# Logarithms and exponentials of the stick-breaking mixer: each kind behind the whole of the other, in a program ordered by its own planner

## The chip, the cores and the metric

The kernel runs on one core of a Trainium2 chip. The metric is the device time of one execution in microseconds, the median of several runs. The engines are PE (TensorE, matrix products, PEld its weight loads), DVE (VectorE, elementwise), ACT (ScalarE, functions by table, and copies), POOL (GpSimd, hardly used) and SP (SyncE, which issues the transfers). Each engine takes its instructions in the order of its own list.

## The reference

A trunk of two layers over 256 positions of width 1024. Each layer is a SwiGLU block, a mixer, and a second SwiGLU block, each with a residual and a layer norm. The mixer of layer 0 is a recurrence (RWKV-7); that of layer 1 is stick-breaking attention over 12 heads. Both are joined with attention over 256 memory tokens. The part that the change touches:

```python
for blk in range(seq // Q_BLOCK):            # two blocks of 128 queries
    ...
    z = jnp.einsum('bhtd,bhsd->bhts', q[:, :, start:end], kb).astype(jnp.float32) * scale
    ...
    log_keep = jnp.where(before, -jax.nn.softplus(z), 0.0)
    later = lax.cumsum(log_keep, axis=3, reverse=True) - log_keep
    att = jnp.where(before, jnp.exp(jax.nn.log_sigmoid(z) + later), 0.0)
    outs.append(jnp.einsum('bhts,bhsd->bhtd', att.astype(v.dtype), vb))
```

All is float32.

## The kernel before

**Tiling.** The 256 positions are two halves of 128, one per partition. Weights arrive by SP in pieces of 128 x 1024 (512 KB, tiles `raw`). ACT copies each piece to fp32r (`hi`), DVE subtracts to get the rest (`lo`), and a product is made of three PE instructions of 512 columns: hi x hi, hi x lo, lo x hi. The activations are held turned in `xTh` and `xTl`. Ten `raw`, nine `hi` and nine `lo` buffers go round. One half's mixer runs beside SwiGLU work of the other half, so that PE has wide products to do while the mixer's chain is on ACT and DVE.

**The stick-breaking mixer** (function `stick`, called once per half). The first half has one block of keys (the diagonal one), the second has two. Scores `z` go to the tiles `qr` (diagonal block) and `Sk` (earlier block). The softplus is taken as max(z, 0) + ln(1 + exp(-|z|)), in tiles of two pairs of heads' scores, 128 x 768: `L` and `Lm` for the diagonal block, `T` and `Tt` for the earlier one. So there are two such tiles in the first half and four in the second, and for each one: ACT takes the absolute value, ACT takes exp(-x) (the *first exponential*), ACT takes ln(1 + x) (the *logarithm*), DVE combines it with the scores (a SCALAR_TENSOR_TENSOR). Then, in groups of 384 columns, PE sums along the keys by a product with a triangular constant (`cst` in the lists), in the second half plus a product with ones of the diagonal block's tile, into the two PSUM banks `ps_2r` and `ps_3r` (tag `tp`); DVE subtracts that from the scores in place; ACT takes the exponential in place (the *last exponential*). Last come the products with the values (`gup_108r`, `vn`), and then the products with `w_out`.

**What sets the order.** The program is recorded first and ordered afterwards, by the class `Plan`. `order` is a list scheduler: each instruction has a price, and at each step it takes for some engine the ready instruction of lowest rank. For ACT it keeps which table is loaded, by the list `SETS` of line 119: an instruction whose function is not in the present set is ranked later by `SWITCH` (line 426) and priced 1300 ns more (line 438). `latest` works due times from the end backwards, and `improve` repeats both 24 times with random shakes of the due times and keeps the best by the planner's own sum. So the prices of one place can change the order of the whole program. Which table each instruction then really needs is settled later, when the program is built, and there a load (ACT_TABLE_LOAD) is put ahead of an instruction whose function the loaded table lacks.

In `stick`, `x.after` lists instructions that have to stand ahead of `x`. Before the change each logarithm stands behind `done`, the last of the half's first exponentials in the order of recording (line 1358), and each last exponential behind `ln`, the last recorded logarithm.

All instructions are issued from line 599, so rows are told apart by their tiles (`L_374r` is the tile `L`, `qr_408r` the scores of the diagonal block). In the lists `ps_` are PSUM banks, `h` the SwiGLU's gated values, `hT` these values turned.

Of the kernel before, what the change touches and what calls it, by code (L numbers as in the profile page):

```python
# [16 lines left out]
AF = mybir.ActivationFunctionType  # L17
# [98 lines left out]
        return lambda *a, **k: self.plan.add(self.name, getattr(self.real, method), method, a, k)  # L116


SETS = (("Exp", "Tanh"), ("Sigmoid", "Tanh"), ("Ln", "Exp"), ("Silu", "Tanh"))
LINK = 45.0  # L120
AGAIN = 32.0
LAND = 3200.0
# [8 lines left out]
class Plan:  # L131
# [214 lines left out]
    def order(self, given=()):  # L346
# [50 lines left out]
        while done < len(ops):  # L397
# [25 lines left out]
            def rank(x):  # L423
                t, o = x
                p = o.pri + (t - t_e) * WAIT
                if e == "ACT" and o.func and o.func not in SETS[table]:
                    p += SWITCH
# [9 lines left out]
            took = o.took  # L437
            if e == "ACT" and o.func and o.func not in SETS[table]:
                table = next(i for i, s in enumerate(SETS) if o.func in s)
                took += 1300.0  # L440
# [162 lines left out]
def kernel(ctx, tc, const, x, mem, f1g, f1u, f1d, f2g, f2u, f2d, ln_g, ln_b, w_out, w_mem_kv,  # L603
                      rw_in, r_mu, r_w0, r_wup, r_a0, r_aup, r_gup, r_kk, r_ka, r_rk, r_lng, r_lnb, sb_in, out):
    nc = Plan(tc.nc)
# [8 lines left out]
    def new(pool, shape, dtype, tag, name, bufs=1):  # L614

        return nc.slot(pool, shape, dtype, tag, nm(name), bufs)

    def ps(tag):
        return new(psp, [P, 512], F32, tag, "ps", 2)
# [9 lines left out]
    def bc(ap, axis, shape):  # L629
        return ap.unsqueeze(axis).to_broadcast(shape)  # L630
# [44 lines left out]
    def split_T(src_ps, dst, j0, n):  # L675

        hi, lo = dst
        sp = src_ps[:, :n * P].rearrange("p (k t) -> p k t", t=P)
        nc.scalar.activation(hi[:, j0:j0 + n], sp, AF.Copy)
        nc.vector.tensor_sub(lo[:, j0:j0 + n], sp, hi[:, j0:j0 + n].bitcast(F32))  # L680
# [209 lines left out]
    def sl(n, shape=None):  # L890
        return new(mp, shape or [P, MIX], F32, n, n)

    def project(hf, w, c0, n):

        a = ps("gu")
        run(cols_mm(a[:, :n], xT[hf], cols_pieces(w, c0, n)))
        t = new(tp_, [P, n], F32, "ta", "pn", 2)
        nc.copy(t, a[:, :n])
        return t

    def turned(src, i0, n):
        pt = ps("tp")
        with nc.together():
            for i in range(n):
                nc.tensor.transpose(pt[:, i * P:(i + 1) * P], src[:, (i0 + i) * P:(i0 + i + 1) * P], ident)
        return pt[:, :n * P].rearrange("p (i t) -> p i t", t=P)
# [396 lines left out]
    def stick(hf, res):  # L1303
        ac = f"acc{hf}"
        qT = sl("bn", [P, NT, P])
        if hf == 0:
            kT = new(cp, [P, NT, P], F32, "S", "kT0")
            V = new(cp, [P, MIX], F32, "gup", "V0")
        else:
            kT, V = sl("kn", [P, NT, P]), sl("vn")  # L1310
        B[hf] = kT, V
        t = project(hf, sb_in[0], 2048, 512)
        nc.copy(V[:, 512:768], t[:, 0:256])
        mq = new(mp, [P, 2, P], F32, "mq", "mq")
        nc.copy(mq, turned(t, 2, 2), 0.125)
        yield "p"
        t = project(hf, sb_in[0], 0, 512)
        nc.copy(qT[:, 0:4], turned(t, 0, 4), 0.125)
        yield "p"
        t = project(hf, sb_in[0], 512, 512)  # L1320
        tv = turned(t, 0, 4)
        nc.copy(qT[:, 4:6], tv[:, 0:2], 0.125)
        nc.copy(kT[:, 0:2], tv[:, 2:4])
        yield "p"
        t = project(hf, sb_in[0], 1024, 512)
        nc.copy(kT[:, 2:6], turned(t, 0, 4))
        yield "p"
        t = project(hf, sb_in[0], 1536, 512)
        nc.copy(V[:, 0:512], t)
        yield "p"  # L1330
        mem_attention(hf, mq)
        zs, sps = {}, {}
        v3 = lambda t: t.rearrange("q (i t) -> q i t", i=3)
        for si, ts in enumerate(range(hf, -1, -1)):
            zm = zs[ts] = sl("qr" if si == 0 else "Sk", [P, 4, 384])
            sps[ts] = [sl(n, [P, 2, 384]) for n in (("L", "Lm") if si == 0 else ("T", "Tt"))]
            for jg in range(2):
                banks = [ps(ac) for _ in range(2)]
                with nc.together():
                    for i in range(3):  # L1340
                        for p in range(2):
                            pr, j = slice(p * HD, (p + 1) * HD), 3 * jg + i
                            nc.tensor.matmul(banks[p][:, i * P:(i + 1) * P], B[ts][0][pr, j], qT[pr, j], start=True, stop=True)
                for p, z in enumerate(banks):
                    g = 2 * jg + p
                    if ts == hf:
                        nc.vector.tensor_tensor(v3(zm[:, g]), v3(z[:, :384]), bc(K_("neg"), 1, [P, 3, P]), ALU.add)
                    else:
                        nc.copy(zm[:, g], z[:, :384])
                    yield "z0"  # L1350
                e, zz = sps[ts][jg], zm[:, 2 * jg:2 * jg + 2]
                nc.scalar.activation(e, zz, AF.Abs)
                done = nc.scalar.activation(e, e, AF.Exp, scale=-1.0)
                yield "z1"
        for ts in zs:
            for jg in range(2):
                e, zz = sps[ts][jg], zs[ts][:, 2 * jg:2 * jg + 2]
                ln = nc.scalar.activation(e, e, AF.Ln, bias=1.0)
                ln.after.append(done.i)
                nc.vector.scalar_tensor_tensor(e, zz, 0.0, e, ALU.max, ALU.add)  # L1360
            yield "ln"
        for ts in zs:
            for g in range(4):
                zm = zs[ts][:, g]
                cu = ps("tp")
                nc.tensor.matmul(cu[:, :384], K_("tri"), sps[ts][g // 2][:, g % 2], start=True, stop=ts == hf)
                if ts != hf:
                    nc.tensor.matmul(cu[:, :384], K_("ones"), sps[hf][g // 2][:, g % 2], start=False, stop=True)
                nc.vector.tensor_sub(zm, zm, cu[:, :384])
                nc.scalar.activation(zm, zm, AF.Exp).after.append(ln.i)  # L1370
                yield "e0"
                yield "e1"
        tss = sorted(zs)
        for g in range(2):
            o = ps(ac)
            ov = o[:, :384].rearrange("p (i t) -> p i t", i=3)
            yield "o"
            with nc.together():
                for i in range(3):
                    for ts in tss:  # L1380
                        for p in range(2):
                            h = 6 * g + 2 * i + p
                            nc.tensor.matmul(ov[p * HD:(p + 1) * HD, i], B[ts][1][:, h * HD:(h + 1) * HD],
                                             zs[ts][:, 2 * g + p, i * P:(i + 1) * P], start=ts == tss[0], stop=ts == tss[-1])
            split_T(o, xT[hf], 3 * g, 3)
        res.append(None)
# [45 lines left out]
    for hf in range(NHALF):  # L1432
        xs[hf] = xp.tile([P, D], F32, tag=f"x{hf}", name=nm("x"))
        nc.in_turn("load", nc.sync.dma_start(xs[hf], x[0, half_sl(hf), :]))
        turn_x(hf)
    for i in range(DEPTH):
        mixer, steps = ((rwkv, RW), (stick, SB))[i % 2]
        last = i == DEPTH - 1
        lag1, lag2 = LAGS[i]
# [60 lines left out]
```

## Time and profile before

| | |
|---|---|
| median of 3 runs | 1111.25 us (1110.56 to 1112.19) |
| the profiled execution's own time | 1110.33 us |
| its span, first to last instruction | 1108.5 us |
| PE busy | 1068.3 us (96%) |
| DVE busy | 928.6 us (84%) |
| ACT busy | 760.0 us (69%) |
| table loads on ACT | 19, 24.4 us, 1283 ns each |
| mean granted clock of PE | 0.988 |
| read from HBM | 301.08 MB, mean 273 GB/s |

A row of a timeline has the start in us, the time it took, the engine, the instruction with what it writes and reads, how often it stands in a row, and in brackets the idle time of that engine before it and what ended it. Starts of PE's instructions that follow each other closely overlap: the distance of two starts is what an instruction costs PE. The granted clock is the share of 2.4 GHz that PE was given: 1.00 is 2.4 GHz, 0.50 is 1.2 GHz.

### The profile page before, as it was taken

The numbers are of one execution on the slowest core, as the hardware profiler recorded it, in microseconds if no ns is written. First come the engines' busy times: TensorE is split into PE (matmuls) and PEld (weight loads), VectorE is DVE, ScalarE is ACT, GpSimd is POOL, SyncE is SP. The second block draws the span as 40 slices with busy tenths as digits, with TensorE's granted clock in tenths as the row PEclk, the third lists the DMA queues.
The fourth block names the chain that finished last, engine by engine and source line by source line (L and its number), as shares of the span: only waits on it lengthen the run. The fifth ranks groups of instructions, "written<-read, shape, count | busy, mean of one in ns | idle before, by whom it ended". The sixth has DMA issues, their size and how long they took to land.

```text
span 1108.5 us, 17727 instructions
## 1 busy us (share of the span) xinstructions
PE 1068.3 (96%) x6265; PEld 862.6 (78%) x6265; DVE 928.6 (84%) x1312; ACT 760.0 (69%) x1027; POOL 2.7 (0%) x14
## 2 busy tenths in 40 slices
PE   7999999998799999999999999999999998999996
PEld 6878888876687778778888888888867876888885
DVE  6578677999999999998789865659899878997777
ACT  6466556986379785686667654538988899866652
POOL 0000000000000000000000000000000000000000
PEclk9999999999999999999999999999999998999998
DMA  9499758865678687799979976758979975999881
GB/s 330 158 360 383 255 211 293 294 211 195 192 236 315 206 282 251 242 319 364 329 264 368 346 230 201 220 172 303 373 249 333 344 252 189 384 371 304 267 286 58
DMA packets 212250, 303.30 MB, mean 274 GB/s; under 512 B 13844, under 2 KB 159424, under 8 KB 212162
## 3 DMA queue, kind: packets, MB, share of 16 engines
q1 hardware_dynamic: 212162, 302.18, 79.9%
q8 instruction: 49, 0.80, 0.3%
q14 instruction: 39, 0.32, 0.1%
HBM read 301.08 MB, written 1.05 MB: 273 GB/s over the span
## 4 chain that ended last, share of the span: by engine, by line
PE 79%; DVE 11%; ACT 4%; DMA 3%; issue 2%; SPq 0%; DVEq 0%; ACTq 0%
PE ps_30r L599 25%; PE ps_29r L599 23%; PE ps_27r L599 7%; PE ps_28r L599 6%; PE ps_25r L599 6%; PE ps_26r L599 6%; PE ps_2r L599 3%; PE ps_3r L599 3%; DVE x L599 1%; DVE Y_369r L599 1%; DVE lo_44r L599 1%; DMA raw_21r<-in_ffn_w_up_dram 1%; DVE lo_17r L599 1%; ACT L599 1%; DVE lb_498r L599 1%
## 5 line engine op out<-in xcount | busy, mean ns | idle before, releaser
L599 ACT ACTIVATE h_31r<-ps_30r 128x256 f32<-128x256 f32 (+1 forms) x38 | 16.5, 435 | 18.5 <-PE ps_30r L599 18.3
L599 ACT ACTIVATE h_32r<-ps_29r 128x256 f32<-128x256 f32 (+1 forms) x38 | 16.2, 425 | 18.9 <-PE ps_29r L599 18.9
L599 ACT ACT_TABLE_LOAD x19 | 24.4, 1283 | 1.1 <-PEq L1488 0.7
L599 PE MATMUL ps_30r<-hi_10r,xTh 128*128 128x512 f32 (+1 forms) x60 | 23.6, 393 | 0.0
L599 PE MATMUL ps_30r<-hi_10r,xTl 128*128 128x512 f32 (+1 forms) x60 | 23.0, 383 | 0.0
L599 PE MATMUL ps_30r<-lo_11r,xTh 128*128 128x512 f32 (+1 forms) x60 | 22.9, 382 | 0.0
L599 PE MATMUL ps_29r<-hi_16r,xTh 128*128 128x512 f32 x56 | 22.8, 407 | 0.0
L599 PE MATMUL ps_30r<-hi_22r,xTh 128*128 128x512 f32 x56 | 22.8, 406 | 0.0
L599 ACT ACTIVATE h_32r<-ps_30r 128x256 f32<-128x256 f32 (+1 forms) x19 | 7.7, 406 | 21.7 <-PE ps_30r L599 21.7
L599 PE MATMUL ps_30r<-hi_13r,xTh 128*128 128x512 f32 x54 | 22.0, 408 | 0.0
L599 PE MATMUL ps_30r<-hi_22r,xTl 128*128 128x512 f32 x56 | 21.9, 391 | 0.0
L599 PE MATMUL ps_29r<-hi_16r,xTl 128*128 128x512 f32 x56 | 21.9, 391 | 0.0
L599 PE MATMUL ps_29r<-lo_17r,xTh 128*128 128x512 f32 x56 | 21.9, 391 | 0.0
L599 PE MATMUL ps_30r<-lo_23r,xTh 128*128 128x512 f32 x56 | 21.8, 390 | 0.0
L599 PE MATMUL ps_30r<-lo_14r,xTh 128*128 128x512 f32 x54 | 21.2, 392 | 0.4 <-DVE lo_14r L599 0.4
L599 PE MATMUL ps_30r<-hi_13r,xTl 128*128 128x512 f32 x54 | 21.2, 393 | 0.0
L599 PE MATMUL ps_29r<-hi_10r,xTh 128*128 128x512 f32 x52 | 21.2, 408 | 0.0
L599 PE MATMUL ps_29r<-lo_44r,xTh 128*128 128x512 f32 x50 | 19.8, 396 | 1.3 <-DVE lo_44r L599 1.3
L599 PE MATMUL ps_2r<-cst,x 128*128 128x128 f32 x48 | 8.9, 315 | 12.6 <-DVE x L599 7.0
L599 PE MATMUL ps_30r<-hi_7r,xTh 128*128 128x512 f32 x50 | 20.7, 414 | 0.0
L599 PE MATMUL ps_29r<-hi_19r,xTh 128*128 128x512 f32 x52 | 20.6, 397 | 0.0
L599 PE MATMUL ps_30r<-lo_17r,xTh 128*128 128x512 f32 x50 | 19.6, 392 | 0.9 <-DVE lo_17r L599 0.9
(1886 smaller groups left out, 4073.1 us busy)
## 6 DMA issues: line engine op xcount, KB each, us to landing
raw_45r<-in_ffn_w_down_dram SPq DMA_DIRECT2D x17, 512.0 KB, 5.8
raw_24r<-in_ffn_w_down_dram SPq DMA_DIRECT2D x16, 512.0 KB, 5.0
raw_15r<-in_ffn_w_down_dram SPq DMA_DIRECT2D x16, 512.0 KB, 5.0
raw_21r<-in_ffn_w_down_dram SPq DMA_DIRECT2D x15, 512.0 KB, 5.8
raw_39r<-in_ffn_w_gate_dram SPq DMA_DIRECT2D x30, 256.0 KB, 4.6
raw_39r<-in_ffn_w_up_dram SPq DMA_DIRECT2D x30, 256.0 KB, 4.4
raw_42r<-in_ffn_w_gate_dram SPq DMA_DIRECT2D x30, 256.0 KB, 5.1
raw_42r<-in_ffn_w_up_dram SPq DMA_DIRECT2D x30, 256.0 KB, 6.1
```

What stands on the lines that cost most here:

```text
L599: fn(*[at(x) for x in a], **{n: at(x) for n, x in k.items()})
```

## The change

The third entry of `SETS` loses the exponential, so that the planner counts a table switch between a logarithm and an exponential. Every logarithm now stands behind all first exponentials of its half, and every last exponential behind all logarithms of its half.

```diff
-SETS = (("Exp", "Tanh"), ("Sigmoid", "Tanh"), ("Ln", "Exp"), ("Silu", "Tanh"))
+SETS = (("Exp", "Tanh"), ("Sigmoid", "Tanh"), ("Ln",), ("Silu", "Tanh"))
...
-        zs, sps = {}, {}
+        zs, sps, first, logs = {}, {}, [], []
...
                 nc.scalar.activation(e, zz, AF.Abs)
-                done = nc.scalar.activation(e, e, AF.Exp, scale=-1.0)
+                first.append(nc.scalar.activation(e, e, AF.Exp, scale=-1.0).i)
...
-                ln = nc.scalar.activation(e, e, AF.Ln, bias=1.0)
-                ln.after.append(done.i)
+                logs.append(nc.scalar.activation(e, e, AF.Ln, bias=1.0))
+                logs[-1].after += first
...
-                nc.scalar.activation(zm, zm, AF.Exp).after.append(ln.i)
+                nc.scalar.activation(zm, zm, AF.Exp).after += [o.i for o in logs]
```

What it makes of the order, at three places. The first is ACT in the second half of the stick-breaking mixer, layer 1, before the change, from the first table load of that stage on. The rows are the logarithm of `L`, the first exponential of `Lm`, the absolute value of `T`, the logarithm of `Lm`, the first exponential of `T` and the logarithm of `Tt`:

```order
L599 ACT_TABLE_LOAD
L599 ACTIVATE L_374r<-L_374r 128x768
L599 ACT_TABLE_LOAD
L599 ACTIVATE Lm_359r<-Lm_359r 128x768
L599 ACTIVATE hT_1994r<-ps_3r 128x256
L599 ACTIVATE T_368r<-Sk_373r 128x768
L599 ACT_TABLE_LOAD
L599 ACTIVATE Lm_359r<-Lm_359r 128x768
L599 ACT_TABLE_LOAD
L599 ACTIVATE T_368r<-T_368r 128x768
L599 ACT_TABLE_LOAD
L599 ACTIVATE Tt_358r<-Tt_358r 128x768
```

And of the changed program, from the same load on; the four in-place rows of 768 are the four logarithms, the last row the first three of the last exponentials:

```order
L599 ACT_TABLE_LOAD
L599 ACTIVATE L_374r<-L_374r 128x768
L599 ACTIVATE hT_1994r<-ps_2r 128x256
L599 ACTIVATE Lm_359r<-Lm_359r 128x768
L599 ACTIVATE T_368r<-T_368r 128x768
L599 ACTIVATE hi_10r<-raw_45r 128x1024
L599 ACTIVATE Tt_358r<-Tt_358r 128x768
L599 ACTIVATE hi_16r<-raw_42r 128x1024
L599 ACTIVATE hi_19r<-raw_18r 128x1024
L599 ACT_TABLE_LOAD
L599 ACTIVATE h_31r<-ps_30r 128x256
L599 ACTIVATE qr_408r<-qr_408r 128x384 x3
```

The first exponentials of `Lm` and `T` and the absolute value of `T` have moved ahead of the load, and the four logarithms stand together.

The second place is DVE beside it, before the change, from the combine of `L` on (`qr_408r<-qr_408r,ps_2r` is the subtraction that empties a bank):

```order
L599 SCALAR_TENSOR_TENSOR L_374r<-qr_408r,L_374r 128x768
L599 TENSOR_TENSOR hT_1994r<-ps_3r,hT_1994r 128x256
L599 SCALAR_TENSOR_TENSOR Lm_359r<-qr_408r,Lm_359r 128x768
L599 SCALAR_TENSOR_TENSOR Tt_358r<-Sk_373r,Tt_358r 128x768
L599 TENSOR_TENSOR qr_408r<-qr_408r,ps_2r 128x384
L599 SCALAR_TENSOR_TENSOR h_32r<-h_32r,ps_30r 128x256
L599 TENSOR_TENSOR qr_408r<-qr_408r,ps_3r 128x384
```

And of the changed program:

```order
L599 SCALAR_TENSOR_TENSOR L_374r<-qr_408r,L_374r 128x768
L599 TENSOR_TENSOR hT_1994r<-ps_2r,hT_1994r 128x256
L599 SCALAR_TENSOR_TENSOR Lm_359r<-qr_408r,Lm_359r 128x768
L599 SCALAR_TENSOR_TENSOR T_368r<-Sk_373r,T_368r 128x768
L599 TENSOR_TENSOR lo_11r<-raw_45r,hi_10r 128x1024
L599 TENSOR_TENSOR qr_408r<-qr_408r,ps_3r 128x384
L599 TENSOR_TENSOR qr_408r<-qr_408r,ps_2r 128x384
L599 SCALAR_TENSOR_TENSOR Tt_358r<-Sk_373r,Tt_358r 128x768
```

The combine of `Tt` has moved behind the first two subtractions, and the combine of `T` and a weight piece stand ahead of them.

The third place is PE in the first half of layer 0's mixer, where `bn_434r` and then `Lm_359r` are turned (products with `cst`, here the identity) through the same two banks, before the change:

```order
L599 MATMUL ps_2r<-cst,bn_434r 128x128 x4
L599 MATMUL ps_30r<-hi_40r,xTh 128x512
L599 MATMUL ps_30r<-lo_41r,xTh 128x512
L599 MATMUL ps_30r<-hi_40r,xTl 128x512
L599 MATMUL ps_2r<-cst,bn_434r 128x128 x2
L599 MATMUL ps_2r<-cst,Lm_359r 128x128 x4
```

And of the changed program:

```order
L599 MATMUL ps_26r<-qr_408r,bn_434r 64x128
L599 MATMUL ps_2r<-cst,bn_434r 128x128 x6
L599 MATMUL ps_2r<-cst,Lm_359r 128x128 x4
L599 MATMUL ps_3r<-cst,Lm_359r 128x128 x2
L599 MATMUL ps_2r<-cst,h_31r 128x128 x2
```

The three wide products between the first four and the last two transposes of `bn_434r` have moved ahead of them.

## Rows read from the trace of the kernel before

**Rows 1.** The page: busy time, share of the span and instructions of each engine.
```profile
PE 1068.3 (96%) x6265; PEld 862.6 (78%) x6265; DVE 928.6 (84%) x1312; ACT 760.0 (69%) x1027; POOL 2.7 (0%) x14
```

**Rows 2.** Waits of PE: who waited for whom, us in total, times, longest.
```profile
PE ps_2r L599 <- DVE qr_408r L599: 5.0, 1, 5.0
PE ps_3r L599 <- DVE L_374r L599: 2.6, 1, 2.6
```

**Rows 3.** Timeline of ACT, 904 to 927 us: start, us, instruction.
```profile
904.35 1.28 ACT L599 ACT_TABLE_LOAD   x1
905.65 0.85 ACT L599 ACTIVATE L_374r<-L_374r 128x768 f32<-128x768 f32 x1
906.51 1.28 ACT L599 ACT_TABLE_LOAD   x1
907.81 0.85 ACT L599 ACTIVATE Lm_359r<-Lm_359r 128x768 f32<-128x768 f32 x1
...
915.29 0.84 ACT L599 ACTIVATE Tt_358r<-Tt_358r 128x768 f32<-128x768 f32 x1
...
926.35 1.35 ACT L599 ACTIVATE qr_408r<-qr_408r 128x384 f32<-128x384 f32 x3
```

**Rows 4.** Timeline of DVE, 906 to 924 us.
```profile
906.53 0.96 DVE L599 SCALAR_TENSOR_TENSOR L_374r<-qr_408r,L_374r 128x768 f32<-128x768 f32 x1
...
916.16 0.96 DVE L599 SCALAR_TENSOR_TENSOR Tt_358r<-Sk_373r,Tt_358r 128x768 f32<-128x768 f32 x1 [3.35 <-ACT Tt_358r L599]
917.04 0.55 DVE L599 TENSOR_TENSOR qr_408r<-qr_408r,ps_2r 128x384 f32<-128x384 f32 x1
...
923.02 1.22 DVE L599 TENSOR_TENSOR lo_38r<-raw_18r,hi_37r 128x1024 fp32r<-128x1024 f32 x1
```

**Rows 5.** Timeline of PE, both halves of the stick-breaking mixer.
```profile
826.45 1.65 PE L599 MATMUL ps_3r<-L_374r,cst 128*128 128x384 f32 x2 [2.57 <-DVE L_374r L599]
...
910.49 0.81 PE L599 MATMUL ps_2r<-L_374r,cst 128*128 128x384 f32 x2
...
917.64 1.65 PE L599 MATMUL ps_2r<-Lm_359r,cst 128*128 128x384 f32 x2 [5.01 <-DVE qr_408r L599]
...
923.96 0.81 PE L599 MATMUL ps_3r<-T_368r,cst 128*128 128x384 f32 x2
924.60 0.81 PE L599 MATMUL ps_3r<-L_374r,cst 128*128 128x384 f32 x2
...
935.25 0.40 PE L599 MATMUL ps_27r<-hi_40r,xTh 128*128 128x512 f32 x1
```

**Rows 6.** Stretches: length; PE, PEld, DVE, ACT, POOL busy; clock; DMA share, GB/s.
```profile
826.40:832.00 5.60, 5.34 (x20) 2.73 (x20) 5.04 (x15) 4.13 (x6) 0.00 (x0) 0.72 0.03 10
912.60:917.60 5.00, 0.03 (x1) 0.00 (x0) 1.63 (x3) 4.93 (x6) 0.00 (x0) 0.73 0.00 0
917.60:922.30 4.70, 4.66 (x10) 3.23 (x11) 2.64 (x5) 4.25 (x5) 0.00 (x0) 0.56 0.00 0
940.00:1000.00 60.00, 60.00 (x273) 49.32 (x272) 56.44 (x71) 45.51 (x54) 0.00 (x0) 1.00 1.04 377
255.90:259.20 3.30, 3.20 (x8) 2.24 (x9) 3.30 (x4) 0.61 (x2) 0.00 (x0) 0.54 0.59 197
```

**Rows 7.** Timeline of PE, 888.4 to 889.5 us: after two transposes, wide products.
```profile
888.87 0.48 PE L599 MATMUL ps_30r<-hi_13r,xTh 128*128 128x512 f32 x1
889.18 0.40 PE L599 MATMUL ps_30r<-lo_14r,xTh 128*128 128x512 f32 x1
889.42 0.40 PE L599 MATMUL ps_30r<-hi_13r,xTl 128*128 128x512 f32 x1
```

**Rows 8.** Timeline of PE, 251 to 255 us, first half of layer 0's mixer.
```profile
251.56 0.60 PE L599 MATMUL ps_2r<-cst,bn_434r 128*128 128x128 f32 x4
...
252.85 0.44 PE L599 MATMUL ps_2r<-cst,bn_434r 128*128 128x128 f32 x2
254.55 0.66 PE L599 MATMUL ps_2r<-cst,Lm_359r 128*128 128x128 f32 x4 [1.27 <-ACT kn_338r L599]
```

## The prediction

> **What bounds the kernel now.** I read the page first: TensorE (PE) is busy 96% of the span, the other engines less [rows 1]. So a change pays only where PE itself waits, or where its clock falls. Second, PE's waits: the longest one inside the layers that is not the start or a norm is 5.0 us, for DVE's subtraction into `qr_408r`; a smaller one of its kind is 2.6 us, for `L_374r` [rows 2]. Both stand in the stick-breaking mixer, the larger in its second half, the smaller in its first. Third, the timelines of ACT, DVE and PE around the larger wait.
>
> The reader is to see a chain there. ACT loads a table at 904.35, takes the logarithm of `L_374r` at 905.65, and then changes tables again and again: in 904 to 926 us 8 loads like that of 904.35 stand, 1.28 us each [rows 3], of 19 in the kernel. DVE obeys its own order: it has the combine of `L_374r` at 906.53, but the subtraction from `ps_2r` stands behind the combine of `Tt_358r`, whose logarithm comes only after four more loads, at 915.29; so the combine starts at 916.16 and the subtraction at 917.04 [rows 3, 4]. PE, which needs that bank for `Lm_359r`, stands from 912.6 to 917.64 [rows 2, 5]. In that stretch nothing is transferred, and the granted clock is 0.56 from 917.6 to 922.3 [rows 6], which is 1.2 GHz for most of it, after the idle time; then it is 2.4 GHz again.
>
> **The change part by part.** No instruction that computes is added or removed. The two lists only bind the order: all four logarithms of a half behind all its first exponentials, all last exponentials behind all logarithms, and the planner now counts a switch between the two. ACT and DVE are in order, so no new semaphore wait is needed. The first half had its two loads already and keeps them. In the second half the new order has 2 loads where the old had 8 (19 to 13 in all): 6 x 1.28 = 7.7 us less on ACT, about 8 with the start of the following instruction, since 904.35 to 905.65 is 1.30. On ACT alone this is worth nothing; its worth is the PE wait.
>
> *Term 1, the place itself.* From the first product with `L_374r` at 910.49 to the first product of `w_out` at 935.25 PE has the same 52 rows in both orders (3732 to 3783), so the work is equal and only waiting and clock can differ. The wait is 5.0. In 917.64 to 922.34 PE does two pairs of products of 384 columns and six of 512: at full clock 2 x 0.64 (923.96 to 924.60, rows 5) and 6 x 0.23 (889.18 to 889.42 is 0.24, rows 7), 2.7 us; it took 4.7, so the clock cost 2.0 [rows 5 to 7]. Together 7.0 us.
>
> What is late next? In the new order three ACT operations of 768 columns that stood between the loads (the exponential of `Lm_359r` at 907.81, the absolute value and the exponential of `T_368r`) come ahead of the first load. ACT had no idle time there, so the load slips by 3 x 0.84 = 2.5 us to 906.9. I walk on with durations of rows 3 and 4: logarithm of `L_374r` done at 909.0, DVE's combine (0.96) at 910.1, PE there at 910.5: no wait, with 0.4 us to spare. PE then does two pairs (1.3) and six wide products (1.4) and wants the bank for `Lm_359r` at 913.2. DVE now has ahead of the subtraction the combines of `Lm_359r` and `T_368r` and one weight piece `lo_11r` (1.22, as 923.02), which needs its ACT copy: done at 913.4, subtraction (0.55) at 914.0. PE waits 0.8. Further on every pair of banks has three wide products and another pair ahead of it (0.7 + 1.3 us) against one subtraction and one piece on DVE (0.55 + 1.22), so I add only 0.1: 7.0 - 0.9 = 6.1 us gained. Bounds: 7.0 if nothing stays. The nearest row on the other side is the first half, which has two loads only and still waits 2.6, with the clock at 0.72 in 826.4 to 832.0 [rows 2, 5, 6], that is 5.6 x 0.28 = 1.6 lost: if the second half became like it, the gain is 7.0 - 4.2 = 2.8. I take the walk: in the first half PE came to `L_374r` at 823.9 (826.45 less the wait) with nothing left to do, here it is busy up to 910.5 and has six wide products behind the first two pairs.
>
> Behind the subtractions DVE's weight pieces are queued, and for those SP waits with its next loads. In the old order the transfers had stopped by 912.6 (0 GB/s, rows 6); in the new one the piece `lo_11r` frees a buffer at about 913, so the weights of the next block come no later.
>
> *Term 2, fewer changes of kind on PE.* The planner orders the whole program anew; PE differs from its row 203 on. PE's list changes between fp32 and the split fp32r products 333 times instead of 359: 13 fewer returns. A return costs 889.18 - 888.87 - 0.23 = 0.08 us [rows 7]: 1.0 us gained. Bounds 0 and 1.5 (four entries into another tile shape fewer, 0.1 each).
>
> *Term 3, a new wait.* In layer 0's first half the transposes of `bn_434r` were parted by three wide products, which hid ACT's copy: 251.56 the first four, 252.85 the last two [rows 8]. In the new order all six follow each other, the last two into the bank that the copy still reads. Four take 0.35, so PE would wait from 251.9 to 252.85: 0.9 us lost, beside the 1.3 at 254.55 that stays. Bounds: 0, if ACT comes sooner, and 2.5 if the low clock that follows there (0.54 over 3.3 us, rows 6) lasts as long again.
>
> Other places are dealt anew too: PE's waits in layer 0's mixers are small, like the 1.3 of rows 8, and I count no net change, +-2 us.
>
> Sum: -6.1 - 1.0 + 0.9 = -6.2 us. The profiled execution took 1110.33, the median of the runs is 1111.25; the terms are differences, so I take them from the median: 1105.1 us (1104.1 against the profiled one).
>
> **A rule that speaks against it.** The rows show a load at 906.51 between the logarithm at 905.65 and the exponential at 907.81 [rows 3]. The Trainium skill, "ScalarE: Activation LUTs", Table sets, says that a logarithm followed by an exponential needs one load, since one set has both. By that rule there would be no load to save here. The trace does not agree: it has a load where the rule asks for none.
>
> **The rivals.** First, the place stays half blocked: the first logarithm comes later than my walk by more than its 0.4 us, and PE waits for `L_374r` as in the first half. For it: ACT is full ahead of 904.35. Against: PE has the wide products. Gain 2.8 + 1.0 - 0.9 = 2.9: 1108.3.
>
> Second, the weights become the limit and the gain is given back: in 940 to 1000 us the transfer engines are at 1.04 of their time and 377 GB/s [rows 6]. If PE, now ahead by 6 us, drains the buffers there, it waits that long: 1111.2, no change. Against: PE has no wait there in the trace, and loads also start sooner.
>
> Third, the change doesn't do what it says: the loads between the logarithms and the exponentials come from something else than the mixed order, and none goes: -1.0 + 0.9, 1111.2. Against: the load of rows 3 between the two kinds, and 13 loads in the new list. The rule above would give this case.
>
> Fourth, slower: one new gap in layer 0's first half. If the wait of term 3 and those behind it (254.55) leave PE idle long enough that the clock stays at 1.2 GHz through the transposes and small products that follow, each 2 us of that work cost 1 more. The rows show 3.3 us of it after 255.9. It decides from some 17 us on (8.5 lost, against 6.2 + 2.2); at 25 us the time is 1105.1 + 12.5 = 1117.6. Against: wide products follow there.
>
> Fifth, better: the transposes of layer 0 cost nothing, neither the new 0.9 nor the old 1.3, nor the low clock behind them (3.3 x 0.46 = 1.5): 3.7 more, 1101.4. For it: ACT's list is dealt anew there. Against: the six in a row.
>
> **How the numbers follow.** Forecast 0.69, with its own range 1102 to 1108; first rival 0.13, weights 0.05, no effect 0.02, slower 0.05, better 0.06. The range 1101 to 1110 takes in the forecast, the better case and the half-blocked one, and leaves out about 0.12. About 0.2% (2.2 us) is what a measurement can tell from no change. Faster: 0.69 + 0.06 + 0.10 of the 0.13 = 0.85. Same: 0.05 + 0.02 + 0.03 = 0.10. Slower: 0.05.
>
> **What would show it.** Right: 13 table loads; in the second half two, with some 12 us from the first to the first last exponential, where it was 22 (904.35 to 926.35); no PE wait over 1.2 us for `qr_408r`, and a full clock there; a new wait of about 0.9 us for ACT's `kn_338r` near 252. Wrong: a PE wait of 2 us or more for `L_374r` near 910; PE waits for `lo` pieces that wait for transfers in the last 170 us; new waits in layer 0 that sum to more than 4 us.

## The result and the profile after

The changed kernel takes 1101.93 us (median of 4 runs, 1101.54 to 1103.93), the kernel before on the same chip 1110.90 (4 runs, 1109.28 to 1112.19): a ratio of 0.9924, 95% interval 0.9905 to 0.9942. That is 9.0 us faster, where 6.2 were forecast; 1101.93 lies inside the range of 1101 to 1110. The profiled execution spans 1099.8 us, where it was 1108.5.

The page's first lines, engine by engine busy time, share of the span and instructions [rows 1]:

```profile
span 1099.8 us, 17711 instructions
PE 1062.8 (97%) x6265; PEld 861.4 (78%) x6265; DVE 928.8 (84%) x1312; ACT 751.6 (68%) x1021; POOL 2.7 (0%) x14
```

DVE's work is the same; ACT has 8.4 us less, 7.7 of it six table loads, which stand in one row (count, total us, mean ns), where the kernel before had 19 with 24.4 us:

```profile
L599 ACT ACT_TABLE_LOAD x13 | 16.7, 1283 | 0.9 <-PEq L1488 0.7
```

The place is the second half of the stick-breaking mixer. ACT's timeline from the load that stood at 904.35 in [rows 3]:

```profile
904.24 1.28 ACT L599 ACT_TABLE_LOAD   x1
905.54 0.85 ACT L599 ACTIVATE L_374r<-L_374r 128x768 f32<-128x768 f32 x1
906.29 0.37 ACT L599 ACTIVATE hT_1994r<-ps_2r 128x256 fp32r<-128x256 f32 x1
906.55 0.84 ACT L599 ACTIVATE Lm_359r<-Lm_359r 128x768 f32<-128x768 f32 x1
907.29 0.84 ACT L599 ACTIVATE T_368r<-T_368r 128x768 f32<-128x768 f32 x1
...
908.97 0.83 ACT L599 ACTIVATE Tt_358r<-Tt_358r 128x768 f32<-128x768 f32 x1
...
911.71 1.28 ACT L599 ACT_TABLE_LOAD   x1
913.01 0.38 ACT L599 ACTIVATE h_31r<-ps_30r 128x256 f32<-128x256 f32 x1
913.29 1.34 ACT L599 ACTIVATE qr_408r<-qr_408r 128x384 f32<-128x384 f32 x3
```

The logarithm of `Lm` follows that of `L` by 1.0 us. Before, 5.3 us lay between them (905.65 in [rows 3], and this row):

```profile
910.97 0.84 ACT L599 ACTIVATE Lm_359r<-Lm_359r 128x768 f32<-128x768 f32 x1
```

The first of the last exponentials comes 9.05 us after the load instead of 22.0. DVE beside it [rows 4]:

```profile
906.41 0.96 DVE L599 SCALAR_TENSOR_TENSOR L_374r<-qr_408r,L_374r 128x768 f32<-128x768 f32 x1
...
907.62 0.95 DVE L599 SCALAR_TENSOR_TENSOR Lm_359r<-qr_408r,Lm_359r 128x768 f32<-128x768 f32 x1
908.49 0.95 DVE L599 SCALAR_TENSOR_TENSOR T_368r<-Sk_373r,T_368r 128x768 f32<-128x768 f32 x1
909.36 1.22 DVE L599 TENSOR_TENSOR lo_11r<-raw_45r,hi_10r 128x1024 fp32r<-128x1024 f32 x1
910.49 0.55 DVE L599 TENSOR_TENSOR qr_408r<-qr_408r,ps_3r 128x384 f32<-128x384 f32 x1
910.96 0.55 DVE L599 TENSOR_TENSOR qr_408r<-qr_408r,ps_2r 128x384 f32<-128x384 f32 x1
```

All of this is without idle time, and the subtractions are done at 911.5; the first one started at 917.04 before. PE needs the bank at 912.1, so it finds it free [rows 5]:

```profile
909.45 0.81 PE L599 MATMUL ps_3r<-L_374r,cst 128*128 128x384 f32 x2
...
912.13 0.81 PE L599 MATMUL ps_3r<-Lm_359r,cst 128*128 128x384 f32 x2
...
926.63 0.39 PE L599 MATMUL ps_28r<-hi_19r,xTh 128*128 128x512 f32 x1
```

From the first product with `L_374r` to the first product of `w_out` PE took 17.18 us; it was 24.76. No row of PE between them has an idle time. The windows (length, PE busy and rows, granted clock, share and rate of the transfers) show the place, from 1 us after its start on, at the full clock, and behind it the transfers as full as before [rows 6]:

```profile
825.00:831.00 6.00, 4.71 (x24) 1.00 0.14 52
910.40:927.70 17.30, 17.30 (x104) 1.00 0.67 218
935.00:990.00 55.00, 55.00 (x251) 1.00 1.04 377
```

Where the 8.7 us of the span came from, by distances between the same products in both traces: 7.58 in the place (24.76 - 17.18); 1.04 ahead of it (the product with `L_374r` came at 910.49 and comes at 909.45); 0.07 behind it (from `w_out`'s first product to PE's last row 163.91 and 163.84). The gain is kept to the end. The 7.58 is the change's; the 1.04 is of the size by which executions with one and the same list on PE differ up to there (see term 3 below).

### The profile page after: what moved, and what is told of

Same layout as the page of the kernel before. It is cut to its first block, busy times and chain, and to the rows that moved or that the text cites. A ratio compares the mean times of both kernels' runs of the same rounds, so it can differ in the third digit from the quotient of the medians.

```text
span 1099.8 us, 17711 instructions
## 1 busy us (share of the span) xinstructions
PE 1062.8 (97%) x6265; PEld 861.4 (78%) x6265; DVE 928.8 (84%) x1312; ACT 751.6 (68%) x1021; POOL 2.7 (0%) x14
## 4 chain that ended last, share of the span: by engine, by line
PE 79%; DVE 13%; DMA 3%; issue 2%; ACT 2%; SPq 0%; DVEq 0%; ACTq 0%
PE ps_30r L599 25%; PE ps_29r L599 24%; PE ps_26r L599 6%; PE ps_25r L599 6%; PE ps_28r L599 6%; PE ps_27r L599 6%; PE ps_2r L599 3%; PE ps_3r L599 3%; DVE x L599 1%; DMA raw_45r<-in_ffn_w_up_dram 1%; DVE lo_44r L599 1%; DVE lb_498r L599 1%; DMA raw_21r<-in_ffn_w_up_dram 1%; DVE lo_20r L599 1%; DVE lo_17r L599 1%
## 5 line engine op out<-in xcount | busy, mean ns | idle before, releaser
L599 ACT ACTIVATE h_32r<-ps_30r 128x256 f32<-128x256 f32 (+1 forms) x35 | 15.1, 431 | 23.1 <-PE ps_30r L599 23.1
L599 ACT ACTIVATE h_31r<-ps_29r 128x256 f32<-128x256 f32 (+1 forms) x34 | 14.5, 426 | 18.5 <-PE ps_29r L599 18.5
L599 PE MATMUL ps_30r<-hi_22r,xTh 128*128 128x512 f32 x64 | 26.3, 410 | 0.0
L599 PE MATMUL ps_30r<-hi_22r,xTl 128*128 128x512 f32 x64 | 25.0, 391 | 0.0
L599 PE MATMUL ps_30r<-lo_23r,xTh 128*128 128x512 f32 x64 | 25.0, 391 | 0.0
L599 PE MATMUL ps_29r<-hi_40r,xTh 128*128 128x512 f32 (+1 forms) x56 | 22.4, 401 | 0.0
L599 PE MATMUL ps_29r<-hi_40r,xTl 128*128 128x512 f32 (+1 forms) x56 | 21.5, 384 | 0.0
L599 PE MATMUL ps_29r<-lo_41r,xTh 128*128 128x512 f32 (+1 forms) x56 | 21.5, 383 | 0.0
L599 PE MATMUL ps_30r<-hi_7r,xTl 128*128 128x512 f32 x52 | 20.4, 392 | 0.0
```

The source lines that it names most:

```text
L599: fn(*[at(x) for x in a], **{n: at(x) for n, x in k.items()})
```

## The experiments

Each row is one kernel, timed beside the kernel before. *Loads* is the number of table loads that belong to the second half's mixer (895 to 930 us), *idle* PE's idle time from 905 to 940 us, *place* the distance from the first product with `L_374r` to the first of `w_out`. In the diffs `...` stands for what is left out, and the comments are added here.

| | loads | idle, us | place, us | ratio to before (95%) |
|---|---|---|---|---|
| before | 8 | 5.01 | 24.76 | 1 |
| changed | 2 | 0 | 17.18 | 0.9924 (0.9905 to 0.9942) |
| e3_act | 2 | 0.18 | 18.00 | 0.9932 (0.9920 to 0.9945) |
| e4_dve | 8 | 3.74 | 23.76 | 0.9985 (0.9977 to 0.9994) |
| e5_oneset | 3 | 0 | 17.55 | 0.9931 (0.9919 to 0.9943) |
| e6_loads_back | 8 | 5.97 | 26.13 | 1.0002 (0.9993 to 1.0010) |
| e1_sets | 4 | 0 | 17.87 | 0.9943 (0.9931 to 0.9956) |
| e2_lists | 4 | 0 | 17.53 | 0.9937 (0.9924 to 0.9950) |
| s_before | 6 | 1.39 | 20.33 | 0.9967 (0.9955 to 0.9979) |
| s_after | 2 | 0 | 17.20 | 0.9941 (0.9929 to 0.9952) |
| v1_free | 5 | 0 | 17.40 | 0.9939 (0.9926 to 0.9951) |
| v2_hand | 2 | 0 | 17.18 | 0.9937 (0.9925 to 0.9949) |

Theory A: the loads made the logarithms late, DVE's list made that a wait of PE, and the wait a low clock. Rival B: DVE's list alone. Rival C: the new deal of the whole program, that is, the other order that the planner makes everywhere else.

**e3_act.** The planner's order of before, then ACT's rows of the place moved by hand:

```diff
-        order = self.improve()
+        order = self.by_hand([o for _, _, o in self.improve()])
...
+        for o in early:                  # exp of Lm, abs and exp of T
+            move(o, l0)                  # ahead of the logarithm of L
+        p = next(o for o in rows if out(o) == "hT")
+        for n in ("Lm", "T", "Tt"):
+            move(logs[n], p, True)
+            p = logs[n]
```

> The kernel before with its whole order kept on PE, DVE and SP; only ACT's list differs, in the second half of the stick-breaking mixer: the exponential of Lm, the absolute value and the exponential of T stand ahead of the logarithm of L, and the logarithms of Lm, T and Tt follow it. Two table loads stand there instead of eight. Theory A (the six loads made the logarithms of Lm and Tt late, and DVE and PE stood behind them): 5.5 to 7 us faster than before, the 5.0 us wait of PE for qr_408r at 0.5 or less, the granted clock full there. Rival B (DVE's place of the combine of Tt ahead of the subtractions did it): DVE's list is unchanged, so 0, within 1 us. Rival C (the gain came from the new deal elsewhere in the program): 0, since nothing else is dealt anew.

Ratio 0.9932, that is 7.6 us of 1111.02, a little over A's 5.5 to 7; in the place it is 6.76. One engine's list in one place gives nearly the whole of it. PE's list is unchanged, so the two parts of the loss can be read cleanly: 24.76 - 18.00 = 6.76, of which 5.01 - 0.18 = 4.83 is the wait and 1.9 the clock. B and C fall as explanations of the bulk.

**e4_dve.** The other half of the chain: ACT keeps its eight loads, DVE no longer has the combine of `Tt` ahead of the subtractions.

```diff
+        p = subs[2]
+        for o in [comb["Tt"]] + glu:     # combine of Tt, two products of h_32
+            move(o, p, True)
+            p = o
+        move(comb["T"], subs[3], True)
```

> The kernel before with all lists kept but DVE's, in the same place: the combine of Tt and the two products of h_32 stand behind the first three subtractions from the banks, the combine of T behind the fourth. ACT keeps its eight loads. Theory A (the loads): the wait for Lm falls from 5.0 to about 0.8, but PE then waits 2.6 us for h_32 and 0.7 us for T, whose ACT rows still stand behind the loads; 2 to 4 us faster than before. Rival B (DVE's order alone): 5.5 to 7 us faster. Rival C (new deal elsewhere): 0.

Ratio 0.9985, 1.7 us (0.7 to 2.6): a little under what A gave. PE's timeline shows why:

```profile
913.03 0.91 PE L637 MATMUL ps_2r<-Lm_359r,cst 128*128 128x384 f32 x2 [0.69 <-DVE qr_408r L637]
...
918.50 0.66 PE L637 MATMUL ps_2r<-cst,h_32r 128*128 128x128 f32 x2 [2.53 <-DVE h_32r L637]
...
921.52 0.71 PE L637 MATMUL ps_3r<-T_368r,cst 128*128 128x384 f32 x1
```

The waits are the forecast ones, 0.7 for the bank and 2.5 for `h_32r`, whose tanh stands behind six loads; one of 0.52 for the last exponential of `Sk_373r` (at 928.64) comes on top. The one for `T` does not show, since the six wide products ahead of it ran at a granted clock of 0.72 (918 to 924) and took that long themselves. So a better list on DVE moves the wait on to the next thing that the loads hold.

**e5_oneset.** Not one instruction changes place. Ahead of a logarithm the table is loaded that has both functions:

```diff
+                if o.eng == "ACT" and o.func == "Ln" and not shared:
+                    self.real.scalar.add_instruction(mybir.InstLoadActFuncSet(
+                        name=..., engine=..., act_func_set_id=6))
+                    shared = True
+                elif o.eng == "ACT" and o.func and o.func not in ("Ln", "Exp"):
+                    shared = False
```

> The kernel before, every instruction of every engine in the same order; the one difference is which table is loaded ahead of a logarithm: the table that holds logarithm and exponential together instead of the one with the logarithm. So the exponentials between the logarithms need no load: three loads instead of eight in the second half of the stick-breaking mixer; in the first half the second load moves from ahead of the last exponentials to a later tanh. Theory A (the loads): 6.5 to 8 us faster than before, no PE wait for qr_408r over 0.5 us in the second half. Rival B (order on DVE) and rival C (new deal elsewhere): 0 to 1 us, since no order changes. A fourth possibility: this table costs longer to load or its functions run longer; then the rows of ACT show it.

Ratio 0.9931, 7.7 us. ACT's timeline, with before's order to the row [rows 3]:

```profile
904.07 1.28 ACT L592 ACT_TABLE_LOAD   x1
905.37 0.85 ACT L606 ACTIVATE L_374r<-L_374r 128x768 f32<-128x768 f32 x1
906.12 0.83 ACT L606 ACTIVATE Lm_359r<-Lm_359r 128x768 f32<-128x768 f32 x1
906.85 0.37 ACT L606 ACTIVATE hT_1994r<-ps_3r 128x256 fp32r<-128x256 f32 x1
907.12 0.83 ACT L606 ACTIVATE T_368r<-Sk_373r 128x768 f32<-128x768 f32 x1
907.85 0.84 ACT L606 ACTIVATE Lm_359r<-Lm_359r 128x768 f32<-128x768 f32 x1
908.59 0.83 ACT L606 ACTIVATE T_368r<-T_368r 128x768 f32<-128x768 f32 x1
909.32 0.83 ACT L606 ACTIVATE Tt_358r<-Tt_358r 128x768 f32<-128x768 f32 x1
910.17 1.28 ACT L606 ACT_TABLE_LOAD   x1
```

Logarithm, exponential, logarithm and exponential follow each other with no load between them, each at the 0.83 to 0.85 us of before; this load takes 1.28 too. With no order changed on any engine, the loads alone make 7.21 us of the place (24.76 - 17.55). It also tells what the first half's second load is worth: it has gone from ahead of the last exponentials there to a later tanh, and that half took as long as before (10.60 us from the end of the wide products ahead of it to the first one behind it, in both).

**e6_loads_back.** The changed kernel's own order, with six loads put back:

```diff
+        again = [o.i for _, _, o in order if o.eng == "ACT" and o.func == "Ln"][-4:-1]
...
+                if o.i in again:
+                    self.real.scalar.activation(self.spare, self.source, AF.Exp)
...
```

> The changed kernel in its own order, with an exponential of one element per partition, whose result nothing reads, behind the logarithms of L, Lm and T of the second half: six table loads come back (eight in that place). Theory A (the loads): the wait of PE for Lm comes back at about 6 us (the combines of Lm and T and a weight piece stand ahead of the subtraction on DVE) and the clock falls behind it: 7 to 8 us slower than the changed kernel, that is 1 to 2 us faster than before. Rival C (new deal elsewhere): at most 1 us slower than the changed kernel, 8 us faster than before.

Ratio 1.0002: everything is gone. PE's wait is the forecast one, and the granted clock behind it is 0.54 from 920.5 to 926.6:

```profile
920.54 1.65 PE L600 MATMUL ps_3r<-Lm_359r,cst 128*128 128x384 f32 x2 [5.97 <-DVE qr_408r L600]
```

The loss, 9.0 us of the place (26.13 - 17.18) and 9.2 of the time (1111.13 - 1101.93, medians of two comparisons), is 1 us more than A gave, by the clock: 6.1 us at 0.54 lose 2.8, where I had put 2 at most. C falls here as well: the new deal is kept, and with eight loads it is worth nothing.

**e1_sets and e2_lists.** Each half of the change alone.

```diff
-SETS = (("Exp", "Tanh"), ("Sigmoid", "Tanh"), ("Ln", "Exp"), ("Silu", "Tanh"))
+SETS = (("Exp", "Tanh"), ("Sigmoid", "Tanh"), ("Ln",), ("Silu", "Tanh"))
```

> Only the first half of the change: the third entry of SETS without the exponential, the lists of before kept (a logarithm behind the last recorded first exponential, a last exponential behind the last recorded logarithm). The order that comes of it has four table loads in the second half of the stick-breaking mixer (eight before, two changed; 15 in all), and they stand ahead of the logarithm of L, the exponential of T, the logarithm of T and a tanh; the logarithms of L and Lm stand together, and no load is ahead of what PE needs first. Theory A (what counts is how late the combine of Lm and the subtractions come): nearly the whole gain, 6.5 to 9 us faster than before. Rival D (each load costs its share, 6 loads for 9 us): two thirds, 5 to 6 us. Rival E (both halves of the change are needed): 0 to 3 us.

```diff
+                logs[-1].after += first
...
+                nc.scalar.activation(zm, zm, AF.Exp).after += [o.i for o in logs]
```

> Only the second half of the change: the longer lists, with the third entry of SETS as before, so that the planner still takes logarithm and exponential for one table. The order that comes of it has four table loads in that place too: ahead of the logarithm of L, a tanh, the logarithm of Tt and the last exponentials; the logarithms of L, Lm and T stand together. Theory A: the subtractions do not stand behind a load any more, 6 to 9 us faster than before; the combine of Tt is late, but PE needs it last. Rival D (each load costs its share): 5 to 6 us. Rival E (both halves are needed): 0 to 3 us.

0.9943 (6.3 us of 1110.53) and 0.9937 (7.0), each with no idle time of PE in the place. E falls: one half is enough. Between A and D the time alone does not decide, since 6.3 lies just under A's 6.5 and both intervals reach D's 6 us; the place does: 17.87 and 17.53 with four loads against 17.18 with two, and no wait in any of them. Once the subtractions come in time, the two loads more cost at most 0.7 us.

**s_before and s_after.** Both kernels with another seed of the planner's shakes:

```diff
-SEED = 144
+SEED = 7
```

> The kernel before with another seed of the planner's shakes (7 instead of 144): the whole program is dealt anew with the same rules. Its order has six loads in that place, not eight, and on DVE the first subtraction stands right behind the combine of Lm, not behind that of Tt. Theory A: the wait there is smaller than in before, at most 1 us for the bank plus some 2 to 3 us for T, so 2 to 5 us faster than before, with 2 us either way for the rest of the new deal. Rival C (any new deal moves the time by as much as the change did): 9 us or more away from before in either direction.

> The changed kernel with seed 7 instead of 144. Its order has two loads in that place, the four logarithms together. Theory A: no PE wait there, within 2 us of the changed kernel (7 to 11 us faster than before), and 3 to 6 us faster than the kernel before with the same seed, which has six loads there. Rival C: no fixed sign between the two kernels of this seed.

0.9967 (3.6 us faster than before) and 0.9941 (6.5, where I had put 7 to 11), so the change is worth 2.9 us with this seed, just under the 3 to 6 I gave. The old rules happened on a milder order here: six loads, waits of 1.39 in all, 20.33 us for the place; 3.1 us of that go with the change. So with these two seeds the size of the gain went with the order that the change met. `s_after` is 2.1 us slower than the changed kernel with seed 144, by medians of two comparisons, which their intervals don't part; its place is equal (17.20).

**v1_free and v2_hand.** Two tries at more, in the first half, where PE waits 2.45 us for `L_374r`. The first has the common table and no lists at all:

```diff
-                ln = nc.scalar.activation(e, e, AF.Ln, bias=1.0)
-                ln.after.append(done.i)
+                nc.scalar.activation(e, e, AF.Ln, bias=1.0)
...
-                nc.scalar.activation(zm, zm, AF.Exp).after.append(ln.i)
+                nc.scalar.activation(zm, zm, AF.Exp)
```

> The kernel before with the table that holds logarithm and exponential together loaded ahead of a logarithm, and without both lists: a logarithm may stand right behind its own first exponential, and the planner's third entry of SETS (logarithm and exponential in one table) is now true. Its order takes the logarithm of L much earlier in both halves (in the first half right after a tanh, 11 rows ahead of its place in before) and has five loads in the second half's mixer, all ahead of what PE needs last or early enough. Theory A: no PE wait for the banks in the second half, so 6 to 9 us faster than before; in the first half the wait of 2.6 us for L goes, and if nothing else held PE there, 1 to 2 us more (8 to 11 us faster in all, as fast as the changed kernel or 2 us faster). Rival F (DVE, full with the norm of the other half's rows, sets the end of the first half): the wait for L only moves, and nothing is gained beyond the changed kernel.

The second is the changed kernel with the common table and the two logarithms and combines of the first half ahead of time:

```diff
+        move(l0, turned, True)           # logarithm of L
+        move(l1, ex1, True)              # logarithm of Lm
...
+        move(c0, xs_[0])                 # combines ahead of the additions to x
+        move(c1, xs_[1])
```

> The changed kernel in its own order on PE and SP; in the first half of the stick-breaking mixer ACT loads the table with both functions and takes the logarithm of L six rows earlier and that of Lm right behind its exponential, with no load ahead of the last exponentials; DVE has the two combines ahead of the two additions to x instead of behind them. Only the first half can change. If the loads made PE's wait of 2.45 us for L there: 2 to 2.5 us faster than the changed kernel, first half from the end of the wide products to the first wide product after it 8 us instead of 10.3. Rival F (DVE is full there and the norm ends it): the wait for L goes but comes back behind DVE for the bank, 10 to 10.5 us, the same time as the changed kernel within 0.6 us.

0.9939 and 0.9937: neither beats the changed kernel. F is borne out by PE's own rows. In `v1_free` the wait for `L_374r` in the first half is gone and one of 2.03 us for DVE's combine of `Lm_359r` has come (828.24). In `v2_hand`:

```profile
823.62 0.91 PE L649 MATMUL ps_2r<-L_374r,cst 128*128 128x384 f32 x2 [0.19 <-DVE L_374r L649]
824.37 0.81 PE L649 MATMUL ps_3r<-L_374r,cst 128*128 128x384 f32 x2
828.66 1.65 PE L649 MATMUL ps_2r<-Lm_359r,cst 128*128 128x384 f32 x2 [3.48 <-DVE qr_408r L649]
```

The wait for `L_374r` went from 2.45 to 0.19, and one of 3.48 came for the next bank, whose subtraction stands behind the norm of the other half on DVE. That half took 11.08 us, where the changed kernel took 10.27 and I had expected 10.5 at most: the longer wait was followed by a low clock. By medians of two comparisons `v2_hand` is 1.7 us slower than the changed kernel, where F had put 0.6 at most, but their intervals overlap. So in these two orders DVE holds up what the loads held up. No kernel of the table is faster than the changed one; those at 0.993 to 0.994 can't be told from it.

## Why the prediction was right, point by point

The sign, the place and the chain were right, and e3, e5 and e6 show them one by one. Of the sum (-6.1 - 1.0 + 0.9) terms 1 and 3 were off in size, both towards too small a gain, and of term 2 only a part is seen. So the time, 9.0 us less where 6.2 were forecast, lies 0.07 below the forecast's own 1102 to 1108 and inside the wider 1101 to 1110.

**Term 1, the place: forecast 6.1, measured 7.58.** The 7.0 of wait and clock was right: e3 has 6.76 with 0.18 of wait left, and e5, which has no wait, 7.21, both with before's list on PE. The step that failed is what stays, "ACT had no idle time there, so the load slips by 3 x 0.84 = 2.5 us". Between the absolute value of `L_374r` and the load three rows were indeed added: in e3, where only they move, that stretch grew from 13.22 to 15.56 us and the load came 2.3 us later against PE. But ACT did have idle time just ahead of that stretch, 1.28 us in before,

```profile
884.90 0.39 ACT L599 ACTIVATE xTh<-ps_27r 128x256 fp32r<-128x256 f32 x1 [1.28 <-PE ps_27r L599]
```

and in the changed order the row of that tile does not wait at all:

```profile
882.11 0.39 ACT L599 ACTIVATE h_32r<-ps_29r 128x256 f32<-128x256 f32 x1 [0.16 <-PE ps_29r L599]
...
884.28 0.37 ACT L599 ACTIVATE xTh<-ps_27r 128x256 fp32r<-128x256 f32 x1
```

so the absolute value of `L_374r` comes 20.85 us ahead of PE's product instead of 19.36, and the load 5.21 ahead instead of 6.14: it slipped by 0.9. I had looked back only as far as the first row that moves. Even with the full slip e3's PE waits 0.18, where the walk left 0.8 (on another list of DVE, that of before). Of the 0.82 that the 7.58 has over e3's 6.76, 0.45 goes with e3's short wait, as e5 has the same list on PE and no wait (18.00 - 17.55), and 0.37 is PE's own order (17.55 - 17.18): the products with `L` stand side by side there, and so do those with `Lm`, so some of term 2 fell into the place.

**Term 2, fewer changes of kind: forecast 1.0.** Only the 0.37 in the place is seen. The rest isn't told apart from other deals: counted in the traces, `e2_lists` has 363 changes of kind and `v1_free` 375, against 359 before and 333 in the changed kernel, and their intervals overlap with that of the changed kernel.

**Term 3, the new wait in layer 0: forecast +0.9, measured -0.1.** The wait came where it was said and about as long [rows 8]:

```profile
254.41 0.44 PE L599 MATMUL ps_2r<-cst,bn_434r 128*128 128x128 f32 x2 [0.69 <-ACT kn_338r L599]
255.32 0.66 PE L599 MATMUL ps_2r<-cst,Lm_359r 128*128 128x128 f32 x4 [0.47 <-ACT kn_338r L599]
```

But the 1.27 behind it, which I said would stay, shrank to 0.47: both wait for ACT's copies in a row, so time waited at the first is not waited at the second. 0.69 + 0.47 = 1.16 against 1.27. "No net change" elsewhere held: PE's idle time from 227 to 460 us is 13.99, where it was 13.58, and 1.04 was gained ahead of the place, inside the 2 us either way. Of the 1.04, 0.43 stands already at 52.9 us, where PE's lists are still equal, and 0.66 at the turning of the rows at the start of layer 1 (486.76 and 486.10); 0.33 came in the first half of the stick mixer (10.60 and 10.27), which kept a wait of 2.45 but not the low clock behind it. Executions with one list on PE differ by as much up to the place: e3 and e5 reach `L_374r` 0.52 and 0.28 us sooner than before, e6 2.28 later than the changed kernel. So that the new deal earned the 1.04 is not shown.

**The rivals.** Half blocked: no, no wait is left. The weights as the limit: no, transfers are at 1.04 and 377 GB/s as before and PE does not wait. No loads removed: no, 13. Slower by the clock in layer 0: no, the low clock behind the two waits lasts as long as before, only later (0.54 in 256.7 to 260.0, where it was 0.54 in 255.9 to 259.2). Transposes that cost nothing: no, 1.16 us of waiting stays where 1.27 was, with that low clock behind it; that 1101.93 lies next to this rival's 1101.4 is chance. Of the signs named, the 13 loads, the full clock and the wait for `kn_338r` came (0.69 at 254.4); from the load to the first of the last exponentials it was 9.05 us where some 12 were expected. Of the signs of being wrong, PE's waits for `L_374r` near 910 and for `lo` pieces do not show. New and longer waits in layer 0 do add up to between 4 and 5 us, but others went, so the idle time there is nearly the same; that sign should have asked for the net.

**The rule that was set aside.** The prediction set a rule aside because the trace had a load between a logarithm and an exponential [rows 3]. e5 shows where the two part: with a table loaded that has both functions, the pair runs with no load between; in the kernels before and after, a load stands between them (at 906.51 before, and at 827.05 after), so the table loaded ahead of the logarithm was one without the exponential. The Trainium skill, "ScalarE: Activation LUTs", Table sets, says that a logarithm followed by an exponential needs one load, since one set has both. It speaks of a set that exists, not of the one that is loaded; which that is, the trace tells.

## What to carry to other kernels

A table load cost ACT 1.3 us here, and the kernel little or nothing until PE's next bank stood behind it in DVE's list: in this place eight loads gave 23.8 to 26.1 us, six 20.3, and two to five all 17.2 to 18.0. So count the wait that they make and the low clock behind it, not the loads. When rows are pulled ahead of a step, look for idle time upstream of them before adding their durations to it, and do not add a new wait to an old one for the same engine's rows, since the second shrinks by the first. Where two helpers stand in a row (ACT, then DVE), relieving one shows what the other holds: e4 and `v2_hand` moved the wait and gained little or nothing.

## What the runs showed of the hardware

A load of the table with both functions takes the same 1.28 us as the others, and logarithms and exponentials run from it at the same 0.83 to 0.85 us for 768 columns (e5). An exponential of a single column between two logarithms costs 0.2 us of its own and two loads, 2.8 us in all (e6).

What an idle time of PE costs beyond itself differs for nearly the same wait. In the first half of the stick mixer 2.57 us of waiting were followed by a granted clock of 0.72 [rows 6], 2.45 us in the changed kernel by 1.00, 3.48 us in `v2_hand` by 0.74 (828.6 to 834.5), 2.38 us in `e1_sets` by 0.70 (826.8 to 832.4), 2.37 us in `s_before` by 1.00 (828.5 to 834.1); in the second half 2.53 us by 0.72 (e4), 5.97 us by 0.54 over 6.1 us (e6). Of the five waits of 2.37 to 2.57 us three were followed by some time at 1.2 GHz, two were not; what decides it for so short a wait these runs don't show.
